# The third product's weight sum, high part and low part in halves in four gate blocks

## The chip, the cores and the metric

The kernel runs on one core of a Trainium2 chip. The metric is the device time of one launch in microseconds (us), the median of several timed runs. Beside it there is one execution with the hardware profiler, whose trace gives the start and the length of each instruction.

The engines are named as in the profile: PE is TensorE's matrix multiplication and PEld its weight load, which runs beside the multiplication before it; DVE is VectorE, ACT is ScalarE, POOL is GpSimd, and SP is SyncE, which issues the DMAs (its queue of DMA issues is SPq).

## The reference

One decoder layer for 256 tokens of width 2048, in fp32: a half-step SwiGLU network, a token-mixing part, and a second half-step SwiGLU network. The change touches the two networks only.

```python
def swiglu_ffn(x, w_gate, w_up, w_down):
    return (jax.nn.silu(x @ w_gate) * (x @ w_up)) @ w_down

# D_MODEL = 2048, D_FF = 5632, SEQ = 256
x = x + 0.5 * swiglu_ffn(rms_norm(x, ffn1_norm), ffn1_w_gate, ffn1_w_up, ffn1_w_down)
...                       # projection, recurrent and convolution heads, output projection
x = x + 0.5 * swiglu_ffn(rms_norm(x, ffn2_norm), ffn2_w_gate, ffn2_w_up, ffn2_w_down)
return rms_norm(x, final_norm)
```

## The kernel before

**High and low parts.** TensorE multiplies in fp32r, a form with fewer bits than fp32. To keep fp32's accuracy each operand is split: the high part `hi` is a cast to fp32r by ACT, in two halves of 128x1024, and the low part `lo` is the operand less `hi`, made by DVE, mostly in one instruction of 128x2048. A product of one weight unit (512 rows by 512 columns, held as 128 partitions x 4 blocks x 512) then takes twelve matmuls: eight with `hi` of the weight (against the high and the low part of x) and four with `lo` of the weight (`multiply`). `parts_of` makes both parts of a unit; `splits_of` only reserves the two buffers for them.

**Seven products instead of eight.** A block of the gate, up or down product is worked on as a 2 x 2 arrangement of weight units (`w11`, `w12`, `w21`, `w22`) against 2 x 2 pieces of x, and `seven` makes it with seven products of sums (Strassen's scheme in Winograd's form) instead of eight. The remaining rows of the weight have units `a2`, `a3`, `b2`, `b3`, which are multiplied in the usual way (`usual`, one for each of two halves of the tokens). The weight sums are differences made by DVE in place: `w11 = w12 - w11` for the second product made, later `w11 = w22 - w11` for the third, `w12 = w22 - w12` for the one after, and `w11 = w21 - w11` for the last but one. The products come in the order 0, 4, 5, 6, 2, 3, 1; the "third product" is `product_of(5, ...)`, the fourth is `product_of(6, ...)`. Between the products 4 and 5 stands the usual product of `b2`, between 5 and 6 that of `b3`.

**Banks.** Four PSUM banks hold the results of a block: `a`, `c`, `e` and `d` (in the profile `ps_g_a`, `ps_g_c`, ... for gate, `ps_u_...` for up, `ps_d_...` for down). Bank `a` takes product 0, then 5, then 6; bank `c` takes product 4, and then the usual products add into it. A `snap` is an ACT copy of a bank to SBUF, at a point where the sum so far is wanted by itself: `s5` of bank `c` after product 4 (named `s_g` in the trace, as numbers are left out), `u2` and `u3` of bank `a` after products 5 and 6 (`u_g`). TensorE can add to a bank only after its snap.

**Buffers.** Raw weight units come by DMA, issued by SP in the order of its queue. `w11` and `w12` lie in the pool `kept` (2 buffers); the others go through the pool `raws` with 3 buffers, in the order `b2`, `w22`, `b3`, `a2`, `w21`, `a3`. So `w21` is loaded into the buffer of `b3`, and can be issued when the last reader of `b3`, its `lo`, has run. The names in the trace: `raw_g_2_00` is `w11` of gate block 2, `_01` is `w12`, `_11` is `w22`, `_10` is `w21`, `_21` is `b2`, `_31` is `b3`, `_20` is `a2`, `_30` is `a3`. `lo_g_2_p` with different numbers is the low part of one product after the other, `lo_g_2_x` that of a usual product.

**Blocks.** Each network runs five gate blocks, each followed by its up block (`s` = 0 to 4), and after `s` = 0, 2 and 4 a down product. In the trace the gate blocks with `s` = 2 and 4 begin at about 282 and 530 us (first network) and 1286 and 1534 us (second).

**What sets the order.** A scheduler reads the program and orders each engine's instructions by the time that it expects each to be ready; an engine then runs them strictly in that order. `tc.keep_in_program_order` exempts an instruction from that. The parameter `order` of `seven` is true only in those four gate blocks; there the two low halves of product 4 and the sum `w12 = w22 - w12` keep their program order on DVE. All instructions are issued through a helper class, so nearly all bear its line, L43; weight loads bear L165 and transposing DMAs (of `h`, through `pair`) L208.

Of the kernel before, what the change touches and what calls it, by code (L numbers as in the profile page):

```python
# [14 lines left out]
ALU = mybir.AluOpType  # L15
# [34 lines left out]
def hybrid_block(ctx: ExitStack, tc: tile.TileContext, a: dict, out: bass.AP):  # L50
    nc = tc.nc
    Engine.pinned = False
    dve, act, pe = (Engine(tc, e) for e in (nc.vector, nc.scalar, nc.tensor))
# [29 lines left out]
    def bank(name):  # L83
        return psum.tile([P, 512], F32, tag="ps", name=name)

    def f32(ap):
        return ap.bitcast(F32)
# [71 lines left out]
    def load(src, name, pieces=((0, UK),), loaded=None, kept=False):  # L159
        if kept:  # L160
            raw = extra[1].tile([P, UK, CW], F32, tag="kept", name=f"raw_{name}", bufs=2)
        else:
            raw = raws.tile([P, UK, CW], F32, tag="raw", name=f"raw_{name}")
        for i, e in pieces:
            nc.sync.dma_start(raw[:, i:e, :], src[i * P : e * P].rearrange("(j p) c -> p j c", p=P))  # L165
            if loaded:
                loaded(i)
        return raw

    def splits_of(name):  # L170
        pool, bufs = splits, 2
        if extra:
            turn_of["split"] += 1
            if turn_of["split"] % 3 == 0:
                pool, bufs = extra[0], 1
        hi = pool.tile([P, UK, CW], F32R, tag="hi", name=f"hi_{name}", bufs=bufs)
        lo = pool.tile([P, UK, CW], F32R, tag="lo", name=f"lo_{name}", bufs=bufs)
        return hi, lo, [(hi[:, j, :], lo[:, j, :]) for j in range(UK)]

    def parts_of(raw, name, pieces=((0, 2), (2, UK)), split=None):  # L180
        hi, lo, blk = splits_of(name)
        for i, e in pieces:
            if split:
                split(i)
            act.copy(hi[:, i:e, :], raw[:, i:e, :])
            if split:
                dve.tensor_tensor(lo[:, i:e, :], raw[:, i:e, :], f32(hi[:, i:e, :]), op=ALU.subtract)
        if not split:
            dve.tensor_tensor(lo, raw, f32(hi), op=ALU.subtract)
        return blk  # L190
# [4 lines left out]
    def stationary(tile, t):  # L195

        return [(tile[:, j, t * P : (t + 1) * P], tile[:, j, S + t * P : S + (t + 1) * P]) for j in range(UK)]
# [33 lines left out]
    def multiply(targets, blk, apart=False, middle=None):  # L231


        more = dict(skip_group_check=True) if apart else {}
        for ps, st, begin, _ in targets:
            for j in range(UK):
                pe.matmul(ps, st[j][0], blk[j][0], start=begin and j == 0, stop=False, **more)
                pe.matmul(ps, st[j][1], blk[j][0], start=False, stop=False, **more)
        if middle:
            middle()  # L240
        for ps, st, _, end in targets:
            for j in range(UK):
                pe.matmul(ps, st[j][0], blk[j][1], start=False, stop=end and j == UK - 1, **more)
        if len(targets) == NT:
            onward()
# [159 lines left out]
    def seven(w, rows, cols, sf, xs, name, keep, done, between=None, ready=None, whole=True, order=False):  # L405


        a, c, e, d = (bank(f"ps_{name}_{n}") for n in "aced")

        def get(u, n, kept=False):  # L410
            src = w[u * UK * P : (u + 1) * UK * P, cols[n] : cols[n] + CW]
            return load(src, f"{name}_{u}{n}", kept=kept)

        (r0, r1), two = rows, len(xs) > 1
        w11, first = ready or (get(r0, 0, True), None)
        w12 = get(r0, 1, True)
        b2, w22 = get(xs[0][0], 1), get(r1, 1)
        b3 = get(xs[1][0], 1) if two else None
        a2, w21 = get(xs[0][0], 0), get(r1, 0)
        a3 = get(xs[1][0], 0) if two else None  # L420

        def snap(ps, n):
            s = keep(f"{n}_{name}")
            act.copy(s, ps)
            return s

        def product_of(i, raw, ps, begin=False, end=True, blk=None):
            multiply([(ps, sf[i], begin, end)], blk or parts_of(raw, f"{name}_p{i}"), True)

        def usual(i, raw, n, *targets):  # L430

            blk = parts_of(raw, f"{name}_x{i}{n}")
            multiply([(ps, stationary(xs[i][1], t), b, z) for ps, t, b, z in targets], blk, True)

        product_of(0, w11, a, True, blk=first)
        s1 = None if whole else snap(a, "s1")
        if whole:
            act.copy(d, a)
        hi, lo, blk = splits_of(f"{name}_p4")
        for i in (0, 2):  # L440
            o = slice(i, i + 2)
            dve.tensor_tensor(w11[:, o], w12[:, o], w11[:, o], op=ALU.subtract)
            act.copy(hi[:, o], w11[:, o])
        for i in (0, 2):
            o = slice(i, i + 2)
            ins = dve.tensor_tensor(lo[:, o], w11[:, o], f32(hi[:, o]), op=ALU.subtract)
            if order:
                tc.keep_in_program_order(ins)
        product_of(4, w11, c, True, blk=blk)
        s5 = snap(c, "s5")  # L450
        if between:
            between(0)
        usual(0, b2, 1, (e, 1, True, not two), (c, 0, False, False))
        if between:
            between(1)
        dve.tensor_tensor(w11, w22, w11, op=ALU.subtract)
        product_of(5, w11, a)
        u2 = snap(a, "u2")
        if between:
            between(2)  # L460
        if two:
            usual(1, b3, 1, (e, 1, False, True), (c, 0, False, False))
        ins = dve.tensor_tensor(w12, w22, w12, op=ALU.subtract)
        if order:
            tc.keep_in_program_order(ins)
        product_of(6, w12, a)
        u3 = snap(a, "u3")
        done(1, 1, e, [u3, s5])
        product_of(2, w22, c)
        done(0, 1, c, [u2])  # L470
        usual(0, a2, 0, (d, 0, not whole, False), (a, 1, False, False))
        dve.tensor_tensor(w11, w21, w11, op=ALU.subtract)
        product_of(3, w11, a, end=not two)
        if two:
            usual(1, a3, 0, (a, 1, False, True), (d, 0, False, False))
        done(1, 0, a, [])
        product_of(1, w21, d)
        done(0, 0, d, [] if whole else [s1])

    def ffn(tag, norm, after, opening=False):  # L480
        with (
# [238 lines left out]
            def down(last):  # L720
# [64 lines left out]
                if tag == 1 and m == 5:  # L785
                    prepare()
                seven(
                    wd, (m, n), (2 * CW, CW), sh, [(u, hidden[u]) for u in others], f"d{tag}_{m}", keep, add,
                    within,
# [6 lines left out]
            for s in range(5):  # L796
                cs = (CW + 2 * s * CW, 2 * CW + 2 * s * CW)
                sg = {}

                def total(ps, tiles):  # L800
                    for p in tiles[1:]:
                        dve.tensor_tensor(tiles[0], tiles[0], p, op=ALU.add)
                    if not tiles:
                        return ps
                    dve.tensor_tensor(tiles[0], ps, tiles[0], op=ALU.add)
                    return tiles[0]

                def gate(t, n, ps, tiles):
                    g = total(ps, tiles)
                    sg[t, n] = tiles[0] if tiles else keep(f"z{tag}_{s}")  # L810
                    act.activation(sg[t, n], g, AF.Silu)

                def up(t, n, ps, tiles):
                    dve.tensor_tensor(sg[t, n], total(ps, tiles), sg[t, n], op=ALU.mult)
                    turn_hidden(1 + 2 * s + n, t, sg[t, n], s % 2 == 0)

                def meanwhile(i):
                    if s == 0 and not opening and i != 1:
                        (sums, lambda: normalise(3))[i // 2]()

                seven(wg, (0, 1), cs, sf, xs, f"g{tag}_{s}", keep, gate, meanwhile, ready.pop() if ready else None,
                      s > 0 and (tag, s) != (1, 3), s in (2, 4))
                seven(wu, (0, 1), cs, sf, xs, f"u{tag}_{s}", keep, up)
                if s % 2 == 0:
                    down(s == 4)
# [45 lines left out]
    with tc.tile_pool(name="mixer", bufs=1) as mp, tc.tile_pool(name="mixw", bufs=2) as mw:  # L871
# [176 lines left out]
        def row_factor(u):  # L1048
# [6 lines left out]
        order = [  # L1055
            (lru_x, 0, 0), (lru_x, 0, 1), (sc_c, 3, 0), (lru_gate, 1, 0), (sc_x, 4, 0),
            (lru_gate, 1, 1), (sc_c, 3, 1), (sc_x, 4, 1), (sc_b, 2, 0), (sc_b, 2, 1),
        ]
# [124 lines left out]
```

## Time and profile before

| | |
|---|---|
| median of 3 runs | 1713.93 us (1713.7 to 1714.16) |
| the profiled execution's own time | 1712.3 us |
| its span | 1710.3 us |
| TensorE busy (PE) | 1693.9 us, 99% of the span |
| VectorE busy (DVE) | 1480.0 us, 87% |
| ScalarE busy (ACT) | 1169.9 us, 68% |
| granted TensorE clock | 0.999 |

The span runs from the first to the last instruction of the trace. A row of the timeline has the start, the length of the group, the engine, the line, the operation, result<-inputs (buffer numbers left out), and the number of instructions in the group; in brackets stands how long the engine idled before it, and what released it. In a table of waits, a row names the engine and what it was about to write, behind the arrow whom it waited for, and then the sum, the number of waits and the longest one.

### The profile page before, as it was taken

How to read it: one execution, taken by the hardware profiler on the slowest of the kernel's cores; microseconds unless marked ns; L12 is line 12 of the kernel's file. 1: busy time of each engine (PE TensorE's matmuls, PEld its weight loads, DVE VectorE, ACT ScalarE, POOL GpSimd, SP SyncE). 2: the span in 40 equal slices, each digit the busy share in tenths (PEclk: the TensorE clock that was granted, in tenths of full speed). 3: DMA queues.
4: the chain of work that ended last, by engine and by line, in shares of the span. 5: the costliest groups of instructions: out<-in, count | busy, mean ns of one | idle time of the engine just before them, and what ended most of it. 6: DMA issues, size and time to landing. Idle time of an engine off the chain costs nothing.

```text
span 1710.3 us, 20226 instructions
## 1 busy us (share of the span) xinstructions
PE 1693.9 (99%) x7803; PEld 1412.4 (83%) x7803; DVE 1480.0 (87%) x1297; ACT 1169.9 (68%) x1489; POOL 6.9 (0%) x32
## 2 busy tenths in 40 slices
PE   8999999999999999999999999999999999999997
PEld 6888888888888888888888888888888888888886
DVE  7998988979889879787986679979989888889786
ACT  6767667776567678775655777676667765677864
POOL 1000000000000000000000000000000000000000
PEclk9999999999999999999999999999999999999999
DMA  8666567575567685855555685685666656576753
GB/s 300 206 221 198 197 221 221 190 257 206 184 208 210 225 267 143 244 172 194 174 194 174 220 271 167 205 257 194 226 201 217 223 191 221 197 215 203 249 194 123
DMA packets 235168, 358.43 MB, mean 210 GB/s; under 512 B 66884, under 2 KB 69312, under 8 KB 234944
## 3 DMA queue, kind: packets, MB, share of 16 engines
q1 hardware_dynamic: 234608, 356.03, 64.7%
q8 instruction: 61, 1.00, 0.2%
q10 hardware_dynamic: 144, 1.05, 0.2%
q14 instruction: 35, 0.29, 0.1%
q0 software_dynamic: 320, 0.07, 0.0%
HBM read 339.82 MB, written 2.10 MB: 200 GB/s over the span
## 4 chain that ended last, share of the span: by engine, by line
PE 92%; ACT 3%; DVE 2%; DMA 1%; issue 1%; SPq 0%; DVEq 0%; ACTq 0%
PE ps_d L43 14%; PE ps_in L43 13%; PE ps_g_a L43 9%; PE ps_u_a L43 8%; PE ps_u_c L43 6%; PE ps_d_a L43 5%; PE ps_o L43 5%; PE ps_g_c L43 5%; PE ps_g_d L43 5%; PE ps_d_c L43 3%; PE ps_u_d L43 3%; PE ps_u_e L43 3%; PE ps_g_e L43 3%; PE ps_d_d L43 3%; PE ps_u L43 2%; PE ps_g L43 2%
## 5 line engine op out<-in xcount | busy, mean ns | idle before, releaser
L43 ACT CAST hi_u_p<-raw_u 128x1024 fp32r<-128x1024 f32 x140 | 141.5, 1047 | 52.5 <-DVE raw_u L43 24.7
L43 ACT CAST hi_g_p<-raw_g 128x1024 fp32r<-128x1024 f32 x132 | 133.8, 1047 | 57.6 <-DVE raw_g L43 30.2
L43 DVE TENSOR_TENSOR lo_u_p<-raw_u,hi_u_p 128x2048 fp32r<-128x2048 f32 (+1 forms) x80 | 159.9, 2018 | 14.4 <-ACT hi_u_p L43 13.8
L43 DVE TENSOR_TENSOR lo_g_p<-raw_g,hi_g_p 128x2048 fp32r<-128x2048 f32 (+1 forms) x75 | 151.6, 2030 | 18.7 <-ACT hi_g_p L43 17.9
L43 PE MATMUL ps_d<-hi_d,h 128*128 128x512 f32 x704 | 167.0, 389 | 0.0
L43 PEld LDWEIGHTS ps_d<-hi_d,h 128*128 128x128 f32 x704 | 132.2, 188 | 27.4
L43 PE MATMUL ps_in<-xT_nm,hi_in 128*128 128x512 f32 x640 | 153.1, 391 | 0.0
L43 PEld LDWEIGHTS ps_in<-xT_nm,hi_in 128*128 128x128 f32 x640 | 117.5, 188 | 23.0 <-ACT tha L43 0.3
L43 ACT CAST hi_d_p<-raw_d 128x1024 fp32r<-128x1024 f32 x84 | 86.1, 1048 | 65.7 <-DVE raw_d L43 34.2
L43 DVE TENSOR_TENSOR lo_d<-raw_d,hi_d 128x2048 fp32r<-128x2048 f32 x44 | 100.2, 2289 | 34.7 <-ACT hi_d L43 34.5
L43 ACT CAST hi_in<-raw_in 128x1024 fp32r<-128x1024 f32 x80 | 80.1, 1046 | 59.6 <-PE ps_in L43 46.2
L43 DVE TENSOR_TENSOR lo_in<-raw_in,hi_in 128x2048 fp32r<-128x2048 f32 x40 | 91.3, 2284 | 33.9 <-ACT hi_in L43 33.6
L43 ACT CAST hi_u_x<-raw_u 128x1024 fp32r<-128x1024 f32 x80 | 81.3, 1047 | 37.1 <-PE ps_u_c L43 25.9
L43 DVE TENSOR_TENSOR lo_d_p<-raw_d,hi_d_p 128x2048 fp32r<-128x2048 f32 (+1 forms) x48 | 96.4, 2019 | 7.2 <-ACT hi_d_p L43 6.8
L43 DVE TENSOR_TENSOR raw_u<-raw_u,raw_u 128x2048 f32<-128x2048 f32 (+1 forms) x50 | 92.3, 1862 | 11.2 <-DMA raw_u<-in_ffn_w_up_dram 10.6
L43 ACT CAST hi_d<-raw_d 128x1024 fp32r<-128x1024 f32 x88 | 88.8, 1046 | 18.0 <-PE ps_d_d L43 7.6
L43 DVE TENSOR_TENSOR lo_g_x<-raw_g,hi_g_x 128x2048 fp32r<-128x2048 f32 x40 | 91.4, 2286 | 7.5 <-ACT hi_g_x L43 7.5
L43 ACT CAST hi_g_x<-raw_g 128x1024 fp32r<-128x1024 f32 x80 | 81.2, 1046 | 20.4 <-PE ps_g_c L43 8.6
L43 DVE TENSOR_TENSOR lo_u_x<-raw_u,hi_u_x 128x2048 fp32r<-128x2048 f32 x40 | 91.3, 2283 | 1.2 <-ACT hi_u_x L43 1.1
L43 DVE TENSOR_TENSOR raw_g<-raw_g,raw_g 128x2048 f32<-128x2048 f32 (+1 forms) x46 | 84.9, 1867 | 5.4 <-DMA raw_g<-in_ffn_w_gate_dram 4.8
L43 PE MATMUL ps_d<-lo_d,h 128*128 128x512 f32 x352 | 87.3, 389 | 0.0
L43 PEld LDWEIGHTS ps_in<-xT_nm,lo_in 128*128 128x128 f32 x640 | 82.1, 191 | 3.1
(405 smaller groups left out, 3673.5 us busy)
## 6 DMA issues: line engine op xcount, KB each, us to landing
raw_d<-in_ffn_w_down_dram SPq DMA_DIRECT2D x88, 1024.0 KB, 5.7
raw_u<-in_ffn_w_up_dram SPq DMA_DIRECT2D x87, 1024.0 KB, 5.3
raw_g<-in_ffn_w_gate_dram SPq DMA_DIRECT2D x86, 1024.0 KB, 5.3
raw_in<-in_w_in_dram SPq DMA_DIRECT2D x40, 1024.0 KB, 5.1
raw_o<-in_w_out_dram SPq DMA_DIRECT2D x16, 1024.0 KB, 5.2
xres<-in_x_dram SPq DMA_DIRECT2D x4, 512.0 KB, 7.4
raw_u<-in_ffn_w_up_dram SPq DMA_DIRECT2D x2, 512.0 KB, 9.3
raw_g_first<-in_ffn_w_gate_dram SPq DMA_DIRECT2D x1, 1024.0 KB, 12.0
```

The lines of the kernel that those rows point to most:

```text
L43: ins = getattr(self.engine, name)(*args, **kwargs)
```

## The change

In the four gate blocks with `order`, the sum `w22 - w11` of the third product, its cast and its low part are each made in two halves of 128x1024, as they already are for the second product. The other gate blocks, the up blocks and the down product keep the sum and the low part whole.

```diff
--- before
+++ after
@@ in seven() @@
         usual(0, b2, 1, (e, 1, True, not two), (c, 0, False, False))
         if between:
             between(1)
-        dve.tensor_tensor(w11, w22, w11, op=ALU.subtract)
-        product_of(5, w11, a)
+        if order:
+            hi, lo, blk = splits_of(f"{name}_p5")
+            for i in (0, 2):
+                o = slice(i, i + 2)
+                dve.tensor_tensor(w11[:, o], w22[:, o], w11[:, o], op=ALU.subtract)
+                act.copy(hi[:, o], w11[:, o])
+            for i in (0, 2):
+                o = slice(i, i + 2)
+                dve.tensor_tensor(lo[:, o], w11[:, o], f32(hi[:, o]), op=ALU.subtract)
+            product_of(5, w11, a, blk=blk)
+        else:
+            dve.tensor_tensor(w11, w22, w11, op=ALU.subtract)
+            product_of(5, w11, a)
         u2 = snap(a, "u2")
```

The scheduler also moves other instructions. VectorE in gate block 2 of the first network, from the low halves of the second product to the low part of the third, before the change (each row is an operation, result<-inputs and shape; `z_1` and `h` are results of the block before, which DVE works on in between):

```order
L43 TENSOR_TENSOR lo_g_2_p_2180<-raw_g_2_00_2145,hi_g_2_p_2179 128x1024
L43 TENSOR_TENSOR z_1_1856<-ps_u_1_d,z_1_1856 128x512
L43 TENSOR_TENSOR lo_g_2_p_2180<-raw_g_2_00_2145,hi_g_2_p_2179 128x1024
L43 TENSOR_TENSOR lo_g_2_x_2202<-raw_g_2_21_2149,hi_g_2_x_2201 128x2048
L43 TENSOR_TENSOR h_4_2116<-pair,h_4_2116 128x4x128
L43 TENSOR_TENSOR raw_g_2_00_2145<-raw_g_2_11_2151,raw_g_2_00_2145 128x2048
L43 TENSOR_TENSOR lo_g_2_x_2256<-raw_g_2_31_2153,hi_g_2_x_2255 128x2048
L43 TENSOR_TENSOR lo_g_2_p_2237<-raw_g_2_00_2145,hi_g_2_p_2236 128x2048
```

The same place after the change:

```order
L43 TENSOR_TENSOR lo_g_2_p_2180<-raw_g_2_00_2145,hi_g_2_p_2179 128x1024
L43 TENSOR_TENSOR z_1_1856<-ps_u_1_d,z_1_1856 128x512
L43 TENSOR_TENSOR raw_g_2_00_2145<-raw_g_2_11_2151,raw_g_2_00_2145 128x1024
L43 TENSOR_TENSOR lo_g_2_p_2180<-raw_g_2_00_2145,hi_g_2_p_2179 128x1024
L43 TENSOR_TENSOR lo_g_2_x_2202<-raw_g_2_21_2149,hi_g_2_x_2201 128x2048
L43 TENSOR_TENSOR h_4_2116<-pair,h_4_2116 128x4x128
L43 TENSOR_TENSOR raw_g_2_00_2145<-raw_g_2_11_2151,raw_g_2_00_2145 128x1024
L43 TENSOR_TENSOR lo_g_2_p_2236<-raw_g_2_00_2145,hi_g_2_p_2235 128x1024
L43 TENSOR_TENSOR lo_g_2_x_2258<-raw_g_2_31_2153,hi_g_2_x_2257 128x2048
L43 TENSOR_TENSOR lo_g_2_p_2236<-raw_g_2_00_2145,hi_g_2_p_2235 128x1024
```

The first half of the third product's sum now stands ahead of the second product's second low half, the first low half of the third product stands ahead of the low part of `b3`, and its second low half behind it.

ScalarE at the same place, before, from the work on `h` to the casts of the third product (`ps_g_2_c` is bank `c`):

```order
L43 CAST h_4_2116<-pair 128x4x128
L43 CAST hi_g_2_x_2255<-raw_g_2_31_2153 128x1024
L43 COPY s_g_2_2199<-ps_g_2_c 128x512
L43 CAST hi_g_2_x_2255<-raw_g_2_31_2153 128x1024
L43 COPY pair<-z_1_1837 128x2x512
L43 CAST hi_g_2_p_2236<-raw_g_2_00_2145 128x1024 x2
```

And after:

```order
L43 CAST h_4_2116<-pair 128x4x128
L43 CAST hi_g_2_p_2235<-raw_g_2_00_2145 128x1024
L43 CAST hi_g_2_x_2257<-raw_g_2_31_2153 128x1024
L43 COPY s_g_2_2199<-ps_g_2_c 128x512
L43 CAST hi_g_2_x_2257<-raw_g_2_31_2153 128x1024
L43 COPY pair<-z_1_1837 128x2x512
L43 CAST hi_g_2_p_2235<-raw_g_2_00_2145 128x1024
```

The first cast of the third product moves ahead of the first cast of `b3` and of the copy `s_g`; the second stays where both stood.

SyncE's queue around the start of the down product that follows gate and up block 2 of the first network, before (loads of w_down, and the transposes of `u_g` and `z`):

```order
L208 DMA_TRANSPOSE u_g_2_2308<-pair 128x8x128
L165 DMA raw_d_5_0_4_2757<-in_ffn_w_down_dram 128x4x512
L208 DMA_TRANSPOSE u_g_2_2253<-pair 128x8x128
L165 DMA raw_d_5_0_6_2795<-in_ffn_w_down_dram 128x4x512
L165 DMA raw_d_5_3_3_2842<-in_ffn_w_down_dram 128x4x512
L208 DMA_TRANSPOSE z_2_2411<-pair 128x8x128
L208 DMA_TRANSPOSE z_2_2430<-pair 128x8x128
L165 DMA raw_d_5_3_4_2873<-in_ffn_w_down_dram 128x4x512
```

And after:

```order
L208 DMA_TRANSPOSE u_g_2_2310<-pair 128x8x128
L208 DMA_TRANSPOSE u_g_2_2255<-pair 128x8x128
L165 DMA raw_d_5_0_4_2759<-in_ffn_w_down_dram 128x4x512
L165 DMA raw_d_5_0_6_2797<-in_ffn_w_down_dram 128x4x512
L165 DMA raw_d_5_3_3_2844<-in_ffn_w_down_dram 128x4x512
L208 DMA_TRANSPOSE z_2_2413<-pair 128x8x128
L165 DMA raw_d_5_3_4_2875<-in_ffn_w_down_dram 128x4x512
L208 DMA_TRANSPOSE z_2_2432<-pair 128x8x128
```

The second transpose of `u_g` has passed a load, and a load has passed the second transpose of `z`. The order on TensorE and GpSimd is unchanged.

## The prediction

> **What bounds the kernel now.** I read the page first, then who waited for whom on TensorE, then the timeline of the first changed block, then the same few rows of the other three.
>
> ```profile
> PE 1693.9 (99%) x7803; PEld 1412.4 (83%) x7803; DVE 1480.0 (87%) x1297; ACT 1169.9 (68%) x1489; POOL 6.9 (0%) x32
> ```
> ```profile
> PE ps_g_a L43 <- DVE lo_g_p L43: 1.7, 4, 0.6
> ```
>
> TensorE (PE) is busy 99% of the span, so any time that can be won lies in its few waits. The second row says that it waited four times, 1.7 us in all and 0.6 at most, for a low part of a gate weight. These are the four blocks of the change, and the wait is that of the third product. The first of them, from the timeline (start, duration, engine, result, wait before):
>
> ```profile
> 280.37 2.35 DVE L43 TENSOR_TENSOR raw_g<-raw_g,raw_g 128x1024 f32<-128x1024 f32 x2
> ...
> 283.90 0.69 DVE L43 TENSOR_TENSOR z<-ps_u_d,z 128x512 f32<-128x512 f32 x1
> ...
> 284.65 1.23 DVE L43 TENSOR_TENSOR lo_g_p<-raw_g,hi_g_p 128x1024 fp32r<-128x1024 f32 x1
> ...
> 287.77 1.04 ACT L43 CAST hi_g_x<-raw_g 128x1024 fp32r<-128x1024 f32 x1
> ...
> 288.60 2.29 DVE L43 TENSOR_TENSOR raw_g<-raw_g,raw_g 128x2048 f32<-128x2048 f32 x1
> 288.72 0.57 ACT L43 COPY s_g<-ps_g_c 128x512 f32<-128x512 f32 x1
> ...
> 289.57 1.77 PEld L43 LDWEIGHTS ps_g_c<-hi_g_x,x 128*128 128x128 f32 x8
> ...
> 290.80 2.29 DVE L43 TENSOR_TENSOR lo_g_x<-raw_g,hi_g_x 128x2048 fp32r<-128x2048 f32 x1
> ...
> 293.39 2.29 DVE L43 TENSOR_TENSOR lo_g_p<-raw_g,hi_g_p 128x2048 fp32r<-128x2048 f32 x1 [0.30 <-ACT hi_g_p L43]
> ...
> 293.43 1.98 PE L43 MATMUL ps_g_a<-hi_g_p,xs 128*128 128x512 f32 x8
> ...
> 295.73 0.77 PEld L43 LDWEIGHTS ps_g_a<-lo_g_p,xs 128*128 128x128 f32 x4 [0.76 <-DVE lo_g_p L43]
> ...
> 296.77 1.98 PE L43 MATMUL ps_g_e<-hi_g_x,x 128*128 128x512 f32 x8
> ...
> 298.90 2.29 DVE L43 TENSOR_TENSOR raw_g<-raw_g,raw_g 128x2048 f32<-128x2048 f32 x1 [0.41 <-DVE raw_g L43]
> ...
> 301.11 4.49 DVE L43 TENSOR_TENSOR lo_g_p<-raw_g,hi_g_p 128x2048 fp32r<-128x2048 f32 x2
> ...
> 303.80 0.87 PEld L43 LDWEIGHTS ps_g_a<-lo_g_p,xs 128*128 128x128 f32 x4
> ```
> ```profile
> 302.37 2.72 PE ps_g_a L43 x12
> ```
>
> The sum of the third product starts at 288.60, its low part ends at 295.68 (293.39 + 2.29), and TensorE's load goes 0.05 later, at 295.73. The twelve matmuls of this product take 3.34 us (293.43 to 296.77); the fourth product's twelve take 2.72 in the chain of waits. So this stop costs 0.62 us, 0.29 more than the 0.33 of plain wait that the sum of four contains. The load idled 0.76, so about the first 0.1 of a late load costs the matmuls nothing. I use both below.
>
> **Term 1, the wait that the halves remove.** The four waits cost 1.7 + 4 x 0.29 = 2.9; I take 2.8. With the new order VectorE (DVE) comes to the second low half about 0.4 earlier than the old low part ended, and the first half is ready 3 us before. TensorE's third low matrix is loaded two matmuls later than the first, so nothing is waited for: **-2.8**.
>
> **Term 2, what stands behind the new cast.** ScalarE (ACT) now makes the first high half ahead of hi_g_x and of the copy s_g. One such cast pushes the next start by 0.95 (287.77 to 288.72), and ScalarE had no idle time there. s_g empties the bank c of the second product, and the load at 289.57, whose matmuls add into that bank, waits for it. s_g ended at 289.29; now 290.24, and the load goes at 290.29, 0.72 late: TensorE loses 0.62. The third block had less room:
>
> ```profile
> 1292.92 0.58 ACT L43 COPY s_g<-ps_g_c 128x512 f32<-128x512 f32 x1
> ...
> 1293.55 1.71 PEld L43 LDWEIGHTS ps_g_c<-hi_g_x,x 128*128 128x128 f32 x8
> ```
>
> There the load already went 0.05 after the copy, so I count 0.9. Blocks 2 and 4 are taken like the first: 3 x 0.62 + 0.9 = **+2.8**. The stop removed comes back 6 us earlier in the same block, under another name.
>
> **Term 3, a weight load that starts later.** Before lo_g_x of b3 (290.80) VectorE now also does the first low half. Two half sums take 2.35 where one whole takes 2.29 (+0.06), the low half adds 1.14 (the 1.23 of the row at 284.65, less the 0.09 by which one instruction's end overlaps the next start: 288.60 + 2.29 against 290.80), and about 0.15 is won back: z ended at 284.59, so with that overlap the next could have started at 284.50 instead of 284.65. Together lo_g_x ends 1.05 later. Its end frees the raw buffer into which SyncE loads w21:
>
> ```profile
> 293.12 0.37 SPq L165 DMA_DIRECT2D raw_g<-in_ffn_w_gate_dram  x1
> ```
> ```profile
> raw_g<-in_ffn_w_gate_dram SPq DMA_DIRECT2D x1, 1024.0 KB, 5.3
> ```
> ```profile
> raw_g<-in_ffn_w_gate_dram SPq DMA_DIRECT2D x5, 1024.0 KB, 5.7
> ```
>
> The load was issued right at that end (290.80 + 2.29) and landed 5.3 later, at 298.4; the sum of the last but one product, at 298.90, needs it, and VectorE keeps lo_g_p of the fourth product behind that sum. Issued at 294.17 it lands at 299.5, so the sum starts at 299.6, 0.7 late here; where the sum started right at the landing, it is the whole 1.05. The low part of the fourth product then ends at 303.39 + 0.7 = 304.1, and the load at 303.80 goes 0.35 late: 0.25 lost. The other blocks:
>
> ```profile
> 549.26 4.49 DVE L43 TENSOR_TENSOR lo_g_p<-raw_g,hi_g_p 128x2048 fp32r<-128x2048 f32 x2
> ...
> 552.47 0.87 PEld L43 LDWEIGHTS ps_g_a<-lo_g_p,xs 128*128 128x128 f32 x4
> ```
> ```profile
> 1304.98 4.49 DVE L43 TENSOR_TENSOR lo_g_p<-raw_g,hi_g_p 128x2048 fp32r<-128x2048 f32 x2
> ...
> 1308.01 0.87 PEld L43 LDWEIGHTS ps_g_a<-lo_g_p,xs 128*128 128x128 f32 x4
> ```
> ```profile
> 1553.04 4.49 DVE L43 TENSOR_TENSOR lo_g_p<-raw_g,hi_g_p 128x2048 fp32r<-128x2048 f32 x2
> ...
> 1556.19 0.87 PEld L43 LDWEIGHTS ps_g_a<-lo_g_p,xs 128*128 128x128 f32 x4
> ```
>
> The first of the two low parts ends 2.29 after each start: 551.55, 1307.27, 1555.33. Plus 1.05 and 0.05 that is 0.18, 0.36 and 0.24 after TensorE's loads; less 0.1 each, 0.08, 0.26 and 0.14. Sum **+0.7**.
>
> **Term 4, the same lateness in the up block.** It is carried on: the buffer of w22 is freed later, so the last gate load lands later, and VectorE's next sums follow. In the up block the third product still has its sum in one piece (low part on VectorE, then TensorE's load):
>
> ```profile
> 333.96 2.29 DVE L43 TENSOR_TENSOR lo_u_p<-raw_u,hi_u_p 128x2048 fp32r<-128x2048 f32 x1 [2.12 <-ACT hi_u_p L43]
> ...
> 336.44 0.87 PEld L43 LDWEIGHTS ps_u_a<-lo_u_p,xs 128*128 128x128 f32 x4
> ```
> ```profile
> 582.18 2.29 DVE L43 TENSOR_TENSOR lo_u_p<-raw_u,hi_u_p 128x2048 fp32r<-128x2048 f32 x1 [2.12 <-ACT hi_u_p L43]
> 585.11 0.87 PEld L43 LDWEIGHTS ps_u_a<-lo_u_p,xs 128*128 128x128 f32 x4
> ```
> ```profile
> 1338.37 2.29 DVE L43 TENSOR_TENSOR lo_u_p<-raw_u,hi_u_p 128x2048 fp32r<-128x2048 f32 x1 [2.12 <-ACT hi_u_p L43]
> ```
> ```profile
> 1340.72 0.82 PEld L43 LDWEIGHTS ps_u_a<-lo_u_p,xs 128*128 128x128 f32 x4
> ```
> ```profile
> 1585.54 2.29 DVE L43 TENSOR_TENSOR lo_u_p<-raw_u,hi_u_p 128x2048 fp32r<-128x2048 f32 x1 [2.12 <-ACT hi_u_p L43]
> 1588.83 0.87 PEld L43 LDWEIGHTS ps_u_a<-lo_u_p,xs 128*128 128x128 f32 x4
> ```
>
> Room between low part and load, less 0.05: 0.14, 0.59, 0.01 and 0.95. VectorE is 0.7, 1.05, 1.05 and 1.05 late, TensorE already 0.25, 0.08, 0.26 and 0.14. The rest uncovered is 0.31, 0.38, 0.78 and nothing; less the 0.1 (not in the third, which is at its limit already): 0.2 + 0.3 + 0.8 = **+1.3**.
>
> **Term 5, the down product.** SyncE's queue also changes: the second transpose of u_g comes ahead of a w_down load, and a w_down load ahead of the second transpose of z.
>
> ```profile
> 356.37 0.37 SPq L165 DMA_DIRECT2D raw_d<-in_ffn_w_down_dram  x1
> 358.05 1.25 SPq L208 DMA_TRANSPOSE u_g<-pair  x1
> ```
> ```profile
> 367.83 2.00 ACT L43 CAST hi_d<-raw_d 128x1024 fp32r<-128x1024 f32 x2
> ```
>
> The load of 356.37 goes after 358.05 + 1.25, at 359.3, and lands by 365.0 at 5.7 us; its cast stands at 367.83, which hides it. If the whole delay comes on top of a VectorE that is 1 us late, that cover of 2.8 still stands. The small reordered sums and copies have no row that fixes their price; between 0 and 1 I take **+0.2**, near zero as the one cover that a row shows is wide.
>
> Sum: -2.8 + 2.8 + 0.7 + 1.3 + 0.2 = **+2.2 us**, 0.13%. The profiled execution, 1712.3, would become 1714.5. It lies 1.6 below the median of the timed runs, 1713.93; that becomes **1716.1**. 0.2%, about what a measurement of this kernel can tell from no change, is 3.4 us.
>
> On the price of halving itself: VectorE's two half sums took 2.35 against 2.29 for one. [...]
>
> **The rivals.**
> *The w21 load lands later than 5.3 (slower).* It is now issued 0.7 ahead of the transpose that follows it, no longer 1.7, and five loads around this block have a median of 5.7. Each 0.1 goes straight into terms 3 and 4, four times. From 0.3 more the total passes 3.4; at 5.7 it is 2.2 + 1.6 = 3.8 (1717.7), at 6.0 2.2 + 2.8 = 5.0 (1718.9). For: the chain has no room at the landing. Against: a load issued first mostly keeps its 5.3. Chance 0.27.
> *The lateness is absorbed.* VectorE idles 2.12 ahead of each lo_u_p; if some of that, or a pause like the 0.41 at 298.90, takes it up, terms 3 to 5 vanish and terms 1 and 2 cancel: 1713.9. Against: that 2.12 is a wait for a cast of the late sum. Chance 0.15.
> *The copy s_g isn't late enough to be felt,* and the gain stays: 1713.93 - 2.8 = 1711.1. It needs ScalarE to have idle time ahead of s_g, of which the rows show none. Chance 0.06. That the change does nothing (the second low half, behind lo_g_x, just as late as before) would also need term 2 absent; it is in this chance.
> The forecast has 0.52.
>
> **How the numbers follow.** 1716.1 is the likeliest case. Low end: the absorbed case less about 1 for a part of term 2 not felt, 1712.8; high end: the load at 6.0 us, 1719.0. Faster by over 3.4 needs more than all of term 1: 0.02. Slower by over 3.4 is the first rival: 0.27. Within: 0.71.
>
> **What would show it.** In the profile after: no wait of ps_g_a for lo_g_p at the third product; in its place four waits of ps_g_c for s_g on TensorE, about 0.5 to 0.9 each; the w21 load about 1 us later after the block's start; short waits for lo_g_p (fourth product) and for lo_u_p. I am wrong if ps_g_c does not wait, or if the later waits are missing and the time is below 1713, or if waits in the down product carry more than 1 us.

## The result, and the profile after

The changed kernel takes 1720.5 us (median of 6 runs, 1719.06 to 1721.6) against 1714.05 us before (6 runs, 1713.2 to 1714.46): 1.0036 times as long, with an interval of 1.0026 to 1.0047. It is slower by about 6.4 us. The profiled execution took 1721.6 us, its span is 1719.8 and the granted clock 0.998 (0.999 before), so the clock plays no part. This is the longest of the six, while the profiled execution before (1712.3) was shorter than all six; so the traces lie 9.3 us apart, and their waits add up to more than the medians differ.

The busy row of the page after:

```profile
PE 1697.0 (99%) x7803; PEld 1412.0 (82%) x7803; DVE 1480.4 (86%) x1305; ACT 1169.5 (68%) x1489; POOL 6.9 (0%) x32
```

The work is the same. VectorE has 8 instructions more and is busy 0.4 us longer; ScalarE is busy as before. The loss lies in waits. This is the table of waits of TensorE's weight loads, before and then after (what waited, for whom; sum, number, longest):

```profile
PEld ps_g_a L43 <- DVE lo_g_p L43: 3.5, 5, 1.1
...
PEld ps_d_c L43 <- ACT s_d L43: 0.8, 2, 0.7
PEld ps_u_a L43 <- DVE lo_u_p L43: 0.6, 2, 0.3
```
```profile
PEld ps_u_a L43 <- DVE lo_u_p L43: 4.8, 6, 1.3
PEld ps_d_c L43 <- ACT s_d L43: 3.7, 2, 2.8
...
PEld ps_g_a L43 <- DVE lo_g_p L43: 3.4, 5, 1.0
...
PEld ps_g_c L43 <- ACT s_g L43: 3.2, 4, 0.9
```

The sum for lo_g_p looks unchanged, but it is another product that waits now, the fourth. Four waits for s_g are new, as predicted. The waits for lo_u_p have grown by 4.2 and those for s_d, in the down product, by 2.9. A reader of the table alone would miss the first point; the timeline of the first changed block after shows it (start, length, engine, result, idle time before):

```profile
284.69 1.22 DVE L43 TENSOR_TENSOR raw_g<-raw_g,raw_g 128x1024 f32<-128x1024 f32 x1
...
287.97 1.05 ACT L43 CAST hi_g_p<-raw_g 128x1024 fp32r<-128x1024 f32 x1
...
289.87 0.57 ACT L43 COPY s_g<-ps_g_c 128x512 f32<-128x512 f32 x1
...
290.49 1.69 PEld L43 LDWEIGHTS ps_g_c<-hi_g_x,x 128*128 128x128 f32 x8 [0.77 <-ACT s_g L43]
...
290.90 1.22 DVE L43 TENSOR_TENSOR lo_g_p<-raw_g,hi_g_p 128x1024 fp32r<-128x1024 f32 x1
...
292.03 2.29 DVE L43 TENSOR_TENSOR lo_g_x<-raw_g,hi_g_x 128x2048 fp32r<-128x2048 f32 x1
...
294.23 1.22 DVE L43 TENSOR_TENSOR lo_g_p<-raw_g,hi_g_p 128x1024 fp32r<-128x1024 f32 x1
...
295.85 0.87 PEld L43 LDWEIGHTS ps_g_a<-lo_g_p,xs 128*128 128x128 f32 x4
...
300.24 2.30 DVE L43 TENSOR_TENSOR raw_g<-raw_g,raw_g 128x2048 f32<-128x2048 f32 x1 [1.99 <-DMA raw_g<-in_ffn_w_gate_dram]
...
302.45 4.49 DVE L43 TENSOR_TENSOR lo_g_p<-raw_g,hi_g_p 128x2048 fp32r<-128x2048 f32 x2
...
304.79 0.76 PEld L43 LDWEIGHTS ps_g_a<-lo_g_p,xs 128*128 128x128 f32 x4 [0.83 <-DVE lo_g_p L43]
```
```profile
294.35 0.37 SPq L165 DMA_DIRECT2D raw_g<-in_ffn_w_gate_dram  x1
295.06 1.24 SPq L208 DMA_TRANSPOSE z<-pair  x1
```
```profile
raw_g<-in_ffn_w_gate_dram SPq DMA_DIRECT2D x1, 1024.0 KB, 5.8
```

No load waits for the third product's low part any more (the row at 295.85). TensorE's load into bank c waits 0.77 for s_g. Then the chain of the w21 load follows: issued at 294.35 (293.12 before), landed after 5.8 us (5.3 before), so that VectorE stands idle 1.99 us ahead of the sum that needs it, and the low part behind that sum makes TensorE's load wait 0.83. The up block behind it (VectorE's low part of the third product there, and TensorE's load):

```profile
336.14 2.29 DVE L43 TENSOR_TENSOR lo_u_p<-raw_u,hi_u_p 128x2048 fp32r<-128x2048 f32 x1 [2.12 <-ACT hi_u_p L43]
338.49 0.76 PEld L43 LDWEIGHTS ps_u_a<-lo_u_p,xs 128*128 128x128 f32 x4 [1.15 <-DVE lo_u_p L43]
```

lo_u_p starts 2.2 us later than before (336.14 against 333.96), not 0.7.

The last down product holds the largest single wait. SyncE, ScalarE and TensorE there, before (two fences) and after (three):

```profile
1618.13 4.07 SPq L208 DMA_TRANSPOSE z<-pair  x2
1622.31 11.99 SPq L165 DMA_DIRECT2D raw_d<-in_ffn_w_down_dram  x4
```
```profile
1619.90 1.04 ACT L43 COPY pair<-z 128x1024 uint16<-128x1024 uint16 x1
1620.85 1.04 ACT L43 CAST hi_d<-raw_d 128x1024 fp32r<-128x1024 f32 x1
1621.80 1.37 ACT L43 COPY pair<-z 128x1024 uint16<-128x1024 uint16 x1
```
```profile
1624.84 1.24 SPq L208 DMA_TRANSPOSE z<-pair  x1
1628.11 0.37 SPq L165 DMA_DIRECT2D raw_d<-in_ffn_w_down_dram  x1
1632.89 1.24 SPq L208 DMA_TRANSPOSE z<-pair  x1
1634.23 13.81 SPq L165 DMA_DIRECT2D raw_d<-in_ffn_w_down_dram  x3
```
```profile
1630.61 2.25 ACT L43 COPY pair<-z 128x1024 uint16<-128x1024 uint16 x2 [2.77 <-DMA z<-pair]
```
```profile
1666.40 1.68 PEld L43 LDWEIGHTS ps_d_c<-hi_d_x,h 128*128 128x128 f32 x8 [2.76 <-ACT s_d L43]
```

Before, ScalarE's second copy of z (1619.90, which feeds the second transpose) stood ahead of the copying back of the first one (1621.80, which needs the first transpose landed), and SyncE issued both transposes one after the other. After, the two copies of 1630.61 stand the other way round: the copying back comes first and waits 2.77 us for the first transpose to land. The second transpose then goes at 1632.89, and SyncE's next load of w_down is queued behind it: 1634.23, where the same load went at 1624.25 before. That is 10 us later, while TensorE was some 7 us behind. The wait for s_d comes 32 us after that load; the chain between them is not followed row by row here, and e9 tests the order instead.

### The profile page after: what moved, and what is told of

It is laid out like the page before. It is cut to its first block, busy times and chain, and to the rows that moved or that the text cites. A ratio compares the mean times of both kernels' runs of the same rounds, so it can differ in the third digit from the quotient of the medians.

```text
span 1719.8 us, 20239 instructions
## 1 busy us (share of the span) xinstructions
PE 1697.0 (99%) x7803; PEld 1412.0 (82%) x7803; DVE 1480.4 (86%) x1305; ACT 1169.5 (68%) x1489; POOL 6.9 (0%) x32
## 5 line engine op out<-in xcount | busy, mean ns | idle before, releaser
L43 DVE TENSOR_TENSOR raw_g<-raw_g,raw_g 128x1024 f32<-128x1024 f32 (+1 forms) x50 | 85.7, 1734 | 12.7 <-DMA raw_g<-in_ffn_w_gate_dram 12.6
```

What stands on the lines that cost most here:

```text
L43: ins = getattr(self.engine, name)(*args, **kwargs)
```

## Experiments

Each kernel was timed beside the kernel before on the same chip; three chips were used for e1 to e10. The ratio is to that kernel, with its 95% interval. Times of single runs of one kernel spread by 1 to 6 us, so differences of 1 to 2 us between two experiments are read from the traces and only supported by the medians. The waits are those of TensorE's weight loads in one profiled execution, summed over the span. Those of e3 (1717.04 us) and e7 (1712.82) are the longest executions of their kernels, well above the medians.

| kernel | median, us | ratio (interval) | s_g | lo_g_p | lo_u_p (bank a) | s_d, last down | w21 landing, us |
|---|---|---|---|---|---|---|---|
| before | 1713.4 to 1714.1 | 1 | 0 | 3.5 | 0.6 | none | 5.2 to 5.4 |
| the change | 1720.5 | 1.0036 (1.0026 to 1.0047) | 3.2 | 3.4 | 4.8 | 2.8 | 5.6 to 6.0 |
| e8: the change again | 1720.18 | 1.0043 (1.0029 to 1.0056) | 3.3 | 3.4 | 2.7 | 2.5 | 5.7 to 5.9 |
| e1: casts behind s_g | 1718.72 | 1.0024 (1.0014 to 1.0034) | 0 | 5.6 | 4.0 | none | 5.6 to 5.8 |
| e2: low part alone in halves | 1713.62 | 0.9994 (0.9985 to 1.0003) | 1.1 | 1.0 | 1.8 | none | 5.2 to 5.4 |
| e3: halves in place | 1713.26 | 0.9997 (0.9988 to 1.0006) | 0 | 1.8 | 4.7 | none | 5.6 to 5.7 |
| e4: last block as before | 1717.63 | 1.0015 (1.0007 to 1.0024) | 2.4 | 3.5 | 1.7 | none | 5.5 to 6.0 |
| e5: transpose later | 1718.84 | 1.0028 (1.0018 to 1.0038) | 3.5 | 1.4 | 2.3 | 2.1 | 5.2 to 5.4 |
| e6: low part whole | 1715.38 | 1.0012 (1.0003 to 1.0021) | 3.4 | 0.7 | 3.2 | none | 5.4 to 5.5 |
| e7: low halves in gate and up | 1710.27 | 0.9980 (0.9972 to 0.9989) | 0 | 1.1 | 0.6 | 0.2 | 5.3 to 5.4 |
| e9: order in the down product | 1718.19 | 1.0024 (1.0015 to 1.0033) | 3.4 | 3.1 | 3.9 | none | 5.6 to 5.8 |
| e10: all three mended | 1713.92 | 1.0000 (0.9991 to 1.0009) | 3.3 | 1.4 | 0.6 | none | 5.2 to 5.5 |

For e4 the landing is that of the three changed blocks. In the table a load's wait counts whole, though about its first 0.15 us costs the matmuls nothing: by the starts of the matmuls in the traces, the 0.77 for s_g above delayed them by 0.62, the 0.83 for lo_g_p by 0.68, and the 2.76 for s_d by 2.61.

**e1: the casts behind s_g.** The edit, in the four blocks, on top of the change:

```diff
-                act.copy(hi[:, o], w11[:, o])
+                with tc.issue_after(copies["s5"].ins):     # not before the copy s_g, on ScalarE
+                    act.copy(hi[:, o], w11[:, o])
```

> The change, with the casts of the third product kept behind the copy s_g on ScalarE in the four blocks (VectorE's order as in the change). Theory A (the late w21 load sets the pace of the block; the wait for s_g only takes a part of the same lateness earlier): the four waits of ps_g_c for s_g go (2.7 us), but TensorE then waits that much longer for lo_g_p of the fourth product, 1.1 to 1.4 us in place of 0.4 to 0.7; the time stays within 1 us of the change, 1719.5 to 1721.5. Theory B (the prices of the prediction add): 1720.5 - 2.7 = 1717.8.

The waits for s_g are gone. The table of waits of this kernel:

```profile
PEld ps_g_a L43 <- DVE lo_g_p L43: 5.6, 5, 1.4
PEld ps_u_a L43 <- DVE lo_u_p L43: 4.0, 6, 1.2
```

2.2 us of the 3.2 came back at the fourth product (3.4 to 5.6). The median, 1718.72, lies between the two theories, and its interval overlaps that of the change. So neither holds as stated. The trace speaks for A in the gate blocks: the wait for s_g and the wait at the fourth product are mostly the same lateness, felt earlier or later. These two prices do not add. This run had no wait for s_d in the last down product, though its order there was the changed one; that accounts for more than the 1.8 us by which its median is lower.

**e2: the low part alone in halves.** The sum stays whole, the casts are the same two:

```diff
-        product_of(5, w11, a)                       # in the four blocks
+        for i in (0, 2): act.copy(hi[:, o], w11[:, o])
+        for i in (0, 2): dve.tensor_tensor(lo[:, o], w11[:, o], f32(hi[:, o]), op=ALU.subtract)
+        product_of(5, w11, a, blk=blk)
```

> Of the change only the low part of the third product in halves, in the four blocks; sum and casts as before, and no other instruction moves on any engine. Theory A: the wait for lo_g_p goes (2.5 to 2.8 us), no wait for s_g comes, the w21 load goes when it went before and lands after 5.2 to 5.4 us; some 0.6 comes back in the third up block, which had no room; 1711.3 to 1712.5. Theory C (VectorE and the loads set the pace, and whatever is won at the third product is lost at the fourth): 1713.5 to 1714.5.

The wait for lo_g_p falls from 3.5 to 1.0, and the load lands as before. But the median moves by 0.3 us only: theory C's figure, though not by its mechanism, since almost nothing (0.2 us) is lost at the fourth product. In the profiled run the third up block lost 1.1 us, more than the 0.6 expected. The third gate block waited 1.1 for s_g, which was not expected either: ahead of that block ScalarE waited 1.70 us for a transpose of u_g, 0.20 before, with the same order on every queue. And 0.9 went in an up block that the edit doesn't touch. Whether these waits belong to the edit or to that run stays open; a gain of up to about 2.5 us is within the interval.

**e3: the halves in place.** Sum, casts and low part in halves, VectorE's first half sum kept behind the low part of b2, the casts behind s_g:

```diff
+                tc.keep_in_program_order(dve.tensor_tensor(w11[:, o], w22[:, o], w11[:, o], ...))
+                with tc.issue_after(copies["s5"].ins):
+                    act.copy(hi[:, o], w11[:, o])
```

> Sum, casts and low part of the third product in halves, but each pair of halves where the whole stood on VectorE, and the casts behind s_g and ahead of the copies for the transposes on ScalarE. The w21 load goes as early as before, the transpose of z about 1 us sooner after it. Theory A1 (a transpose that starts sooner behind the load makes it land later): landing 5.6 to 6.0 us, waits of 0.2 to 0.5 at the fourth product, 1713 to 1714.5. Theory A2 (the longer landing comes with the later issue, not with the transpose): landing 5.2 to 5.4 us, and the time of the run with the low part alone in halves, 1711.3 to 1712.5.

SyncE in the first block, and how long the first row's load took to land:

```profile
293.34 0.37 SPq L165 DMA_DIRECT2D raw_g<-in_ffn_w_gate_dram  x1
294.48 1.24 SPq L208 DMA_TRANSPOSE z<-pair  x1
```
```profile
raw_g<-in_ffn_w_gate_dram SPq DMA_DIRECT2D x1, 1024.0 KB, 5.6
```

The load goes about as early as before (293.34 against 293.12), yet lands after 5.6 us, 5.6 to 5.7 in all four blocks. What differs is the transpose, 1.14 us behind the load, no longer 1.73. A1 holds, the time of 1713.26 too. The median itself does not tell e3 from e2; the landings do.

**e4: the last of the four blocks as before.** `if order and name != "g2_4"`.

> The change in three blocks; the fourth gate block (s = 4 of the second network) is as before, and with it the order in the up block and the down product that follow. Theory D (in the last down product the order of SyncE's queue, a transpose of z ahead of a load, costs 2.5 us): the wait of ps_d_c for s_d falls from 2.8 to about 0.7, the time to 1717.5 to 1718.5. Theory E (that loss is carried over from the late blocks before it): the wait stays, 1719.5 to 1721.

The time is D's, 2.9 us below the change for one block of four, and the last down product has no wait for s_d in it. Part of the 2.9 is the block's own loss, so this alone doesn't settle the down product; e9 does.

**e5: the transpose later.** Only one pair of instructions changes places on ScalarE in each of the four blocks, against the change: the copy that feeds the transpose goes behind the snap u2.

```diff
+        with tc.issue_after(held_back[0].ins) if held_back else nullcontext():   # held_back: the snap u2
             act.copy(two.rearrange(flat, b=2), src.bitcast(U16).rearrange(mixed, b=2))
```

> The change, with one thing more in the four blocks: on ScalarE the copy that feeds the transpose behind the w21 load is kept behind the snap of the third product, so that the transpose starts about 4 us after the load, no longer 0.7. Theory A1 (the transpose's traffic makes the load land later): landing 5.0 to 5.3 us instead of 5.6 to 6.0, the waits at the fourth product fall from 0.4 to 0.8 each to 0 to 0.3, and those in the up block by as much or less; 1716.5 to 1718.8. Theory A2 (the landing is long because the load is issued late): 5.6 to 6.0 us still, 1719.5 to 1721.5.

The first block again: load and transpose on SyncE, the landing, the sum that needs the load, and TensorE's load for the fourth product:

```profile
294.54 0.37 SPq L165 DMA_DIRECT2D raw_g<-in_ffn_w_gate_dram  x1
...
298.91 1.24 SPq L211 DMA_TRANSPOSE z<-pair  x1
299.92 2.29 DVE L43 TENSOR_TENSOR raw_g<-raw_g,raw_g 128x2048 f32<-128x2048 f32 x1 [1.47 <-DMA raw_g<-in_ffn_w_gate_dram]
...
304.47 0.76 PEld L43 LDWEIGHTS ps_g_a<-lo_g_p,xs 128*128 128x128 f32 x4 [0.32 <-DVE lo_g_p L43]
```
```profile
raw_g<-in_ffn_w_gate_dram SPq DMA_DIRECT2D x1, 1024.0 KB, 5.3
```

The load is issued as late as in the change and lands after 5.3 us. The wait at the fourth product falls from 0.83 to 0.32, the sum for lo_g_p from 3.4 to 1.4. That settles A1 against A2: it is the transpose close behind the load that stretches the landing (in the first block 5.8 us with the transpose 0.71 behind, 5.3 with it 4.37 behind). The median, 1718.84, is just above what A1 expected, with an interval that overlaps the change's.

**e6: the low part whole.** The change without its second loop: sum and casts in halves, `dve.tensor_tensor(lo, w11, f32(hi), ...)` once.

> The change with the low part of the third product whole again: sum and casts in halves, placed as in the change, so that s_g is late as there, but no low half stands ahead of b3's low part. Theory A (the late w21 load is what costs): the load goes at most 0.4 us later than before and lands after 5.2 to 5.4 us; s_g costs its 2.1 to 2.7, the wait for lo_g_p of the third product is gone for it, nearly nothing is lost at the fourth product; 1713.5 to 1715. Theory H (the halves of the sum and of the cast, which move ahead of other work, are the cost): 1717 to 1720.

s_g costs as much as in the change (3.4), and little is lost at the fourth product (0.7). 1715.38 is 0.4 above A's range and well below H's. So the sum and casts in halves win at the third product about what they cost at s_g; most of the loss comes with the first low half ahead of b3's low part. That includes the down products: without the low halves SyncE's queue has the order of before everywhere. The waits for lo_u_p, 3.2, are more than A named.

**e7: low halves in the gate and up blocks.** e2's edit in the four gate blocks and in the up blocks behind them.

> The low part of the third product in halves in the four gate blocks and in the up blocks behind them, sum and casts whole. Theory A: gains 2.3 to 2.6 us at the third product of the gate blocks and loses nothing in the third up block; 1711.2 to 1712.5. Theory C (the gain is lost again at later waits for loads): 1713 to 1714.5.

```profile
PEld ps_g_a L43 <- DVE lo_g_p L43: 1.1, 4, 0.4
...
PEld ps_u_a L43 <- DVE lo_u_p L43: 0.6, 2, 0.3
```

1710.27, 1 us better than A's best, and the interval lies clear of 1: this version beats both kernels. It moves no instruction on any queue of loads, and at the third product one load only still waits, 0.25 us in the third gate block; the other waits that the two rows count stand at other products.

**e8: the change again.**

> The change itself once more, beside the others on one chip. Theory D (the order of SyncE's queue costs 2.5 us in the last down product): TensorE's wait for s_d there is again 2.5 to 3 us. Theory D0 (that wait depends on how long loads happen to take in a run): under 1.5 us. In both the waits for s_g, for lo_g_p at the fourth product and for lo_u_p are there again, 0.4 to 1 us each, and the time is 1719 to 1721.5.

The wait for s_d was 2.5 us again, as D has it. The waits for s_g and at the fourth product are there too, those for lo_u_p in three of the four up blocks only, so that their sum is 2.7 and not 4.8.

**e9: the order in the down product.** On top of the change, VectorE's low part of the second w_down unit stays behind the sum z:

```diff
+            with tc.issue_after(ahead[0].ins) if second else nullcontext():   # ahead: the last sum z
                 dve.tensor_tensor(lo, raw, f32(hi), op=ALU.subtract)
```

> The change, with one thing more: on VectorE the low part of the second w_down unit is kept behind the sum z of the block before, as it stood before the change. With that the second copy of z stands ahead of the copying back on ScalarE again, and both transposes of z ahead of the load in SyncE's queue. Theory D (the scheduler's new order in the down product costs 2 to 2.5 us, mostly in the last one): no wait of ps_d_c for s_d above 0.9 us in the last down product, 1717 to 1718.5. Theory D0 (that wait comes by chance with slow loads): 1719.5 to 1721.5.

ScalarE and SyncE in the last down product now:

```profile
1629.01 2.30 ACT L43 COPY pair<-z 128x1024 uint16<-128x1024 uint16 x2
```
```profile
1626.28 5.03 SPq L212 DMA_TRANSPOSE z<-pair  x2
1631.42 8.83 SPq L165 DMA_DIRECT2D raw_d<-in_ffn_w_down_dram  x3
```

Both transposes go together again, ahead of the loads, and ScalarE doesn't wait. No wait for s_d is left there, and 1718.19 is inside D's range. With the changed order the last down product waited in 3 profiled runs of 4 (the change, e8, e5; not e1), with the old order above 0.2 us in none of 8. D holds, with the one exception of e1, where the first transpose of z landed 3.2 us after its issue, against 5.7 in the change. In the last down product of the first network the same wait is there with either order: 0.7 to 0.9 us with the old one, but 1.9 in e3, and 0.7 to 1.9 with the changed one; so what e9 shows is clear for the last down product only.

**e10: all three mended.** e5, e9 and e7's edit of the up blocks on top of the change.

> The change with the three things mended that the theory names: the transpose behind the w21 load later, the order of the down product as in the run before it, and the low part of the third product in halves in the up blocks behind the four gate blocks too. Only the late copy s_g stays. Theory A: the gain of 2.3 to 2.8 us at the third product stands against 2.1 to 2.7 us at s_g, and little else is left: 1713 to 1715. If something else that the theory does not name costs time: above 1716.

1713.92, in the middle of the expectation. What is left is the gain at the third product and the price of s_g, which cancel, as the prediction's first two terms said, and 0.7 us at the fourth product.

## Why the prediction was wrong

The forecast, 1716.1 with a range up to 1719.0, was too low, by 4.4 us; its sign was right and its size too small. One of its own signs of being wrong came true: waits in the down product carry more than 1 us.

TensorE runs the same matmuls in the same order in all these kernels, and where nothing waits one starts 0.227 us after the other (the median within the blocks, in the traces of before and of the change). So the starts of the matmuls show where time went. The table has the time of each stretch less that of the same stretch before, in us, from one profiled execution of each kernel:

| stretch | forecast | the change | e8 | e1 | e5 | e9 | e10 |
|---|---|---|---|---|---|---|---|
| third product, four gate blocks | -2.8 | -2.8 | -2.8 | -2.8 | -2.8 | -2.8 | -2.8 |
| where s_g is waited for | +2.8 | 2.7 | 2.8 | 0.0 | 3.0 | 2.9 | 2.9 |
| fourth product | +0.7 | 2.7 | 2.7 | 4.9 | 0.7 | 2.5 | 0.7 |
| the up blocks behind | +1.3 | 4.0 | 1.9 | 3.3 | 1.7 | 3.6 | 0.0 |
| down products | +0.2 | 2.8 | 3.3 | 0.0 | 3.1 | 0.1 | 0.0 |

- **Term 1 (-2.8) was right.** No wait for the third product's low part is left. In the table of waits it can't be seen, since the fourth product's have the same name.
- **Term 2 (+2.8) was right in place and size where s_g is felt:** four waits, 2.7 us. What was wrong is that it stands beside the other terms: by e1 most of it (4.9 in place of 2.7 at the fourth product) would have come back later anyhow.
- **Term 3 (+0.7) was too small.** The step that failed is "landed 5.3 later" being carried over to a load that goes 0.7 us ahead of the transpose. The argument that a load issued first mostly keeps its 5.3 rested on rows in which the transpose came 1.7 us behind it. The first rival had this condition and this distance, and a landing of 5.7 to 6.0; I gave it 0.27. It landed after 5.6 to 6.0. Take 5.8 instead of 5.3: 0.5 more in each block is 2.0, so about 2.7 in all, as measured. With the transpose out of the way (e5, e10) the fourth product loses the 0.7 of the forecast. e3 and e5 show the cause from both sides.
- **Term 4 (+1.3) was too small,** because it took VectorE to be late by what one load gave. The rooms that it read off the rows were right to 0.1 us. But the last gate load, behind w21, took its own time: in the first block it went at 306.97 and took 6.9 us, against 305.62 and 6.0 before, so it landed 2.2 us later, and lo_u_p came 2.2 us late. In the up blocks with the low part whole, of all these kernels, the loss is how much later than before this load landed, less how much later TensorE was, less a room of 0.2, 0.65, 0.05 and 1.0 us in the four blocks, to within 0.05 (nothing where this is below zero). In the change the load took 6.3 to 7.1 us, in e8, the same kernel, 5.9 to 6.9; that is nearly the whole difference between 4.0 and 1.9. That the transpose behind w21 has a part in it is not shown: e5, without it, still loses 1.7. No edit moved the last gate load alone, so the fit is not a test; e10 loses nothing there with the low part in halves.
- **Term 5 (+0.2) was the other failure.** I priced the transpose of u_g that passes a load, and named the one of z without pricing it. A load ahead of a transpose looked harmless. The cost lay behind it: ScalarE's copy for that transpose stood behind a copy that waits for the transpose before it, and a load stood behind the transpose on SyncE. It is 2.8 and 3.3 us in the down products by the traces of the change and of e8. With the old order in e9 it is 0.1, and the distance to the kernel before on the same chip falls from 6.8 us (e8) to 4.3.
- **The rival that ended slower** had the right mechanism and still stopped at 1718.9, because it left the down product as it was.
- **The price of halving** was small, as the row said: in the block above a half of 1.22 us is followed 1.13 after its start (290.90 to 292.03), and in e2 two low halves took 2.36 where one whole takes 2.29. As one starts before the other ends, the second half cost 0.07 us there.

What stays open: why loads of the same name take so different a time from run to run with the same order on every queue (the last gate load of the first block took 6.9 us in the change and 6.3 in e8); and with it how much of the spread of single runs (e6: 1713.42 to 1719.71) and of the difference between e2 and e7 is due to them. Where the low part of the up block is whole, as in e2, the third up block has a room of 0.05 us for that load and lost 1.1 us; in e7 it lost 0.1, but the last up block lost 0.8. Why e2 alone gains so little where e7 gains 3 us is not settled by that.

## What to carry to other kernels

Take the smallest edit that removes the wait, and look at what the scheduler moves with it: halving the low part alone, in gate and up blocks, moved nothing on the queues of loads and won 3 us, while halving sum and cast as well as the low part let the scheduler pull work ahead of the last reader of a load's buffer and of a transpose's copy. When a load has no room at its landing, ask what is issued within its flight, not only when it is issued itself. And waits in one block can share one lateness: in e1, removing the first of them moved most of it to the next.

## What was not expected of the hardware

In these kernels the transpose of 128 x 1024 two-byte elements that the same queue issues behind the 1 MB load of w21 stretches the landing of that load. By distance behind the load: 4.4 us, 5.2 to 5.5 (e5, e10); 1.73, 5.2 to 5.4 (before, e2, e7); 1.3, 5.4 to 5.5 (e6); 1.15, 5.6 to 5.7 (e3); 0.7, 5.5 to 6.0 (the change, e4, e8, e9); 0.47, 5.6 to 5.8 (e1). On the mean of each kernel's blocks that is 5.27 to 5.35 us at 1.73 and more, 5.43 at 1.3, and 5.65 to 5.82 at 1.15 and less. So it cost 0.3 to 0.5 us here where it started within about 1.2 us behind the load, and nothing that can be seen from 1.7 on. The traces don't show by what mechanism.
